# Queries on all partitions: selecting matmuls out of PSUM, or repeated loads from a DRAM scratch

## The chip, the cores and the metric

The kernel runs on one core of a Trainium2 chip. The core has TensorE (matmuls, written PE; its weight loads PEld), VectorE (DVE), ScalarE (ACT), GpSimd (POOL) and SyncE (SP), whose queue issues most of the loads and stores, and 16 DMA engines that carry them out. Each engine works through its own list of instructions in order; semaphores hold an instruction back until what it needs is there. The metric is the device time of one execution in microseconds (us), the median of several.

## The reference

One layer of a decoder step is computed for a prompt of 512 tokens and for a sample group: 8 sequences of 8 new tokens, each with its own cache. The part that matters here is the dilated attention of the sample group, for three groups of four heads with (window, dilation) = (128, 1), (512, 4) and (2048, 16):

```python
def dilated_attention_sample(q, k_ext, v_ext, window, dil, slopes):
    # q: (B,L,Hg,E); k_ext, v_ext: window buffer rows, then the L new rows
    span = window // dil
    jj = np.arange(span + 1)
    idx = wb + np.arange(l_len)[:, None] - jj[None, :] * dil
    ...
    s = jnp.einsum('blhe,bljhe->blhj', q, kg) * (e ** -0.5)
    s = jnp.where(valid[None, :, None, :], s + bias, NEG_INF)
    p, den, lse = _softmax_parts(s, -1)
    o = jnp.einsum('blhj,bljhe->blhe', p, vg) / den
    return o, lse[..., 0]
```

With dilation 16 and 8 new tokens, the token i of a sequence reads the cached rows whose position has residue i modulo 16: 128 keys of four heads of 64 elements. No two of the eight tokens share a cached key. The outputs of the three groups are weighted by a softmax over their denominators and go through further projections.

## The kernel before

The core holds activations with features on the partitions and 576 tokens (512 of the prompt, 64 of the sample group) on the free axis. Nearly all matmuls are projections in `products` (L231): weights and activations are split into a high and a low part of fp32r, and each product is made of three matmuls. Weights come in chunks of 512 KB by SyncE (L164) into three buffers; ScalarE casts the high part (L148) and VectorE subtracts to get the low part (L150). L423 is the same scheme for values that come out with tokens on the partitions.

The attention stage goes over the groups in the order 2, 1, 0. For each it projects the queries, keys and values of all tokens, and then makes the prompt's units (`part_scores`, L833 to L840; `part_values`, L848 to L859) in turn with steps of the sample group, which a generator hands out (`all_samples`). What an engine does in which order is settled when the program is built: a scheduler there puts the instructions of the code into one list for each engine and may draw projections that are written later, such as the gate projections `gc` (written behind the whole stage), between the steps of the attention, where they fill TensorE while it would wait.

Group 2's sample scores (`scores_by_query`) are not made by TensorE, since every token has its own keys. For each quad of sequences `bq` (two) and each token's residue r (eight), `unit` loads a tile `kv` of 128 keys on the partitions by 4 sequences by 256 elements (512 KB, L870). Each half of it (two sequences) is multiplied element by element with the token's query, which must stand on all 128 partitions, and summed over each head's 64 elements into `sT` (L917). TensorE puts the query there: `qhl` holds the queries' rows, token by partition, in a high part on partitions 0 to 63 and a low part on 64 to 127, and `sel` has two ones in each column. A matmul with one column of `sel`, repeated 128 times, as weights (L909) writes the sum of the two rows on all partitions of a PSUM bank. For the first half VectorE multiplies straight out of PSUM (L916); for the second ScalarE copies PSUM into `qr` (L913) and GpSimd multiplies (L914). VectorE makes the sums of both. The tiles `qr` share a tag, and so three buffers, with `skT` of the other groups. Behind the eighth residue, `sT` is transposed (L940), the bias is added and the minimum taken (`minus_max`, L819), ScalarE takes exponentials (L945), and two transposes (L947, L948) turn them for the product with the values (L955, L964). The products are masked into `od` (L968) and summed into `orow` (L969).

At the end of the stage the last quad of group 0 goes through these steps, while the prompt's group weights `ae` are turned by transposes (L1083) and multiplied into the prompt's outputs (L1085); the sample group's weights are applied to `orow` (L1088), three transposes (L1091) turn it, and its parts go into `oun`. From `oun` come the high and low parts `och` and `ocl` (L1113) for the projection behind the stage.

`small()` hands out PSUM banks: in turns, each fifth one by the name h (shared with `held()`) and the others by the name s; in the attention stage only those named s. Line numbers in the text are those of the kernel before, save where the kernel after is spoken of; there they are 5 less in the sample steps (L947 is L942), 10 less from L1027 on, and 1 more in the prompt's units.

Of the kernel before, what the change touches and what calls it, by code (L numbers as in the profile page):

```python
# [104 lines left out]
def hybrid_step(ctx: ExitStack, tc: tile.TileContext, I, O, at_a, at_b):  # L105
# [707 lines left out]
    nat = oup.tile([128, 4, 3, 2, 4], F32, name="nat")  # L813
    stp = oup.tile([128, 4, 2, 2, 4], F32, name="stp")
    scr = dpool.tile([512, 16], F32, name="scr")

    def minus_max(out, scores, bias, least):

# [82 lines left out]
    def scores_by_query(sT, bq):  # L901

        for r in range(NR[2]):
            kt = unit(2, bq, r, 0)
            for half in range(2):
                pq = small()
                for n in range(2):
                    tok = 8 * (4 * bq + 2 * half + n) + r
                    T.matmul(pq[:, 256 * n:256 * n + 256], sel[:, tok:tok + 1].to_broadcast([128, 128]), qhl, start=True, stop=True)  # L909
                k2 = kt[:, 2 * half:2 * half + 2, :].rearrange("p b f -> p (b f)")  # L910
                if half:
                    qr = sa.tile([128, 512], F32, tag="skT", name="qr", bufs=3)
                    S.copy(qr, pq)  # L913
                    G.tensor_tensor(k2, k2, qr, op=OP.mult)  # L914
                else:
                    V.tensor_tensor(k2, k2, pq, op=OP.mult)  # L916
                V.tensor_reduce(sT.rearrange("p (b h i) -> p b h i", b=4, h=4)[:, 2 * half:2 * half + 2, :, r],  # L917
                                k2.rearrange("p (b h e) -> p b h e", b=2, h=4), axis=AX.X, op=OP.add)
            yield
# [71 lines left out]
    for g in GROUPS:  # L991
# [19 lines left out]
        if g == 2:  # L1011
            pt = small()
            for p in range(2):
                qd = sa.tile([128, 2, 64], F32, tag="qd", name="qd", bufs=1)
                for d in range(2):
                    V.tensor_copy(qd[:, d, :], qs[:, 4 + p, :])
                T.transpose(pt[:, 128 * p:128 * p + 128], qd.rearrange("p d n -> p (d n)"), ident)
            qhl = sa.tile([128, 256], F32R, tag="qhl", name="qhl")
            S.copy(qhl, pt[:, :256])
            V.tensor_tensor(qhl[64:128], pt[64:128, :256], qhl[64:128].bitcast(F32), op=OP.subtract)  # L1020
            sel = sa.tile([128, 64], F32R, tag="sel", name="sel")
            V.tensor_tensor(sel, ident[:, 0:64], ident[:, 64:128], op=OP.add)

        for _ in prompt_units(g, qT, kT, vt):
            for _ in range(STEPS[g]):
# [490 lines left out]
```

## Time and profile before

| | us |
|---|---|
| median of 3 runs | 1310.12 (1309.93 to 1310.55) |
| the profiled execution's own time | 1309.6 |
| its span, first to last instruction | 1307.6 |
| TensorE's granted clock, mean | 0.997 |

A row of the profile names the line of the kernel, the engine, the operation and the tiles (out<-in), the count and the durations. Rows of one line give the shortest, median and longest duration in ns, then the first and last start in us. Matmuls overlap in TensorE, so the duration of one is longer than the distance to the next. A chain of waits is read back from the last instruction: each piece is what the end waited for at that time. The busiest lines of the page's second part, the span in 40 slices, show how evenly TensorE is filled (tenths of each slice):

```profile
PE   8899999999999999999999999999999999999996
DMA  7241432376573767355767432563556656545423
```

The attention stage with its sample steps lies in slices 15 to 24.

### The profile page before, as it was taken

Reading aid. Unit: us, or ns where it says so; the run is one execution under the profiler, and the core shown is the slowest. Engines: PE = TensorE matmul, PEld = TensorE weight load, DVE = VectorE, ACT = ScalarE, POOL = GpSimd, SP = SyncE. Lnnn points to the kernel's source line nnn. Section 1 sums busy time; section 2 is a strip of 40 time slices with the busy share of each in tenths; the row PEclk is TensorE's granted clock in tenths of the full one; section 3 lists DMA queues with packets and bytes.
Section 4 is the critical chain, followed back from the end, with each engine's and each line's share of the span. In section 5 each row is a group of like instructions: output and inputs, shape, how many; then the busy total and the mean of one; then the engine's idle time right before and its main releaser. Section 6 shows DMA issues by size and latency. Waiting matters only on the chain.

```text
span 1307.6 us, 24226 instructions
## 1 busy us (share of the span) xinstructions
PE 1279.0 (98%) x9699; PEld 1227.7 (94%) x9699; DVE 685.3 (52%) x1294; ACT 573.1 (44%) x1262; POOL 251.1 (19%) x400
## 2 busy tenths in 40 slices
PE   8899999999999999999999999999999999999996
PEld 6899999999999999998988879999989999999996
DVE  5855564343463223171624357545898888773233
ACT  6554553544432222252533334444456666553333
POOL 4320211013420222041312101022232222200000
PEclk9999999999999999999999999999999999999999
DMA  7241432376573767355767432563556656545423
GB/s 221 65 133 53 146 118 69 97 232 192 163 250 91 244 218 257 95 172 166 227 191 216 139 93 81 157 223 107 160 149 155 138 136 150 116 112 142 137 77 117
DMA packets 225484, 196.39 MB, mean 150 GB/s; under 512 B 8444, under 2 KB 216937, under 8 KB 224596
## 3 DMA queue, kind: packets, MB, share of 16 engines
q1 hardware_dynamic: 218682, 142.28, 37.4%
q0 software_dynamic: 6688, 52.57, 13.4%
q8 instruction: 76, 1.25, 0.4%
q14 instruction: 36, 0.29, 0.1%
q10 hardware_dynamic: 2, 0.00, 0.0%
HBM read 175.52 MB, written 54.27 MB: 176 GB/s over the span
## 4 chain that ended last, share of the span: by engine, by line
PE 83%; issue 5%; DVE 5%; ACT 4%; DMA 2%; SPq 0%; POOL 0%; POOLq 0%; ACTq 0%; DVEq 0%
PE g L231 44%; PE g L1430 8%; PE g L423 7%; PE g L1273 6%; PE s L1273 3%; PE s L1430 2%; DMA wr<-wr 1%; PE h L964 1%; PE s L833 1%; DVE wl L150 1%; PE h L1273 1%; PE s L231 1%; PE s L909 1%; PE s L892 1%; PE s L848 1%
## 5 line engine op out<-in xcount | busy, mean ns | idle before, releaser
L150 DVE TENSOR_TENSOR wl<-wr,wh 128x512 fp32r<-128x512 f32 (+2 forms) x286 | 201.8, 708 | 324.4 <-ACT wh L148 305.4
L231 PE MATMUL g<-xh,wh 128*128 128x288 f32 (+2 forms) x1120 | 334.7, 299 | 3.1 <-DVE ae L1319 1.6
L231 PE MATMUL g<-xh,wl 128*128 128x288 f32 (+2 forms) x1120 | 334.0, 298 | 0.5 <-DVE wl L150 0.5
L231 PE MATMUL g<-xl,wh 128*128 128x288 f32 (+2 forms) x1120 | 332.7, 297 | 0.1
L148 ACT CAST wh<-wr 128x512 fp32r<-128x512 f32 (+2 forms) x290 | 174.8, 607 | 341.4 <-PE g L231 229.8
L231 PEld LDWEIGHTS g<-xh,wh 128*128 128x128 f32 x1120 | 211.8, 189 | 7.3 <-issue 3.8
L231 PEld LDWEIGHTS g<-xh,wl 128*128 128x128 f32 x1120 | 211.6, 189 | 1.8 <-DVE wl L150 0.8
L231 PEld LDWEIGHTS g<-xl,wh 128*128 128x128 f32 x1120 | 211.6, 189 | 1.7 <-issue 1.1
L1233 DVE TENSOR_TENSOR wl<-wr,wh 128x512 fp32r<-128x512 f32 x119 | 81.3, 707 | 22.2 <-ACT wh L1232 22.0
L1232 ACT CAST wh<-wr 128x512 fp32r<-128x512 f32 x119 | 70.3, 620 | 45.5 <-DVE wr L1224 23.1
L423 PE MATMUL g<-wh,xh 128*128 128x256 f32 x224 | 71.1, 318 | 2.8 <-DVE vs L428 2.8
L1430 PE MATMUL g<-hh,wh 128*128 128x288 f32 (+2 forms) x286 | 71.3, 297 | 0.2 <-ACT hh L1244 0.2
L1430 PE MATMUL g<-hh,wl 128*128 128x288 f32 (+2 forms) x286 | 71.2, 297 | 0.0
L423 PE MATMUL g<-wl,xh 128*128 128x256 f32 x224 | 71.1, 318 | 0.0
L423 PE MATMUL g<-wh,xl 128*128 128x256 f32 x224 | 70.9, 317 | 0.0
L1430 PE MATMUL g<-hl,wh 128*128 128x288 f32 (+2 forms) x286 | 70.7, 296 | 0.0
L1273 PE MATMUL g<-xh_t,wh 128*128 128x288 f32 x204 | 60.5, 297 | 0.6 <-DVE h L1366 0.4
L1273 PE MATMUL g<-xh_t,wl 128*128 128x288 f32 x204 | 60.3, 295 | 0.0
L1273 PE MATMUL g<-xl_t,wh 128*128 128x288 f32 x204 | 59.9, 294 | 0.0
L423 PEld LDWEIGHTS g<-wh,xh 128*128 128x128 f32 x224 | 51.6, 230 | 4.1 <-DVE vs L428 3.0
L423 PEld LDWEIGHTS g<-wl,xh 128*128 128x128 f32 x224 | 51.6, 230 | 1.2 <-issue 1.2
L423 PEld LDWEIGHTS g<-wh,xl 128*128 128x128 f32 x224 | 51.6, 230 | 1.2 <-issue 1.2
(520 smaller groups left out, 2987.6 us busy)
## 6 DMA issues: line engine op xcount, KB each, us to landing
wr<-in_w_in_dram SPq DMA_DIRECT2D x74, 512.0 KB
wr<-in_ffn_w_up_dram SPq DMA_DIRECT2D x44, 512.0 KB
out_dram<-in_cache_k_w_dram POOLq DMA_DIRECT2D x8, 2040.0 KB, 9.6
out_dram<-in_cache_v_w_dram POOLq DMA_DIRECT2D x8, 2040.0 KB, 9.8
kv<-in_cache_k_w_dram SPq DMA_DIRECT2D x26, 512.0 KB
kv<-in_cache_v_w_dram SPq DMA_DIRECT2D x26, 512.0 KB
wr<-wr POOLq DMA_DIRECT2D x34, 256.0 KB, 3.7
wr<-in_ffn_w_down_dram SPq DMA_DIRECT2D x18, 448.0 KB
```

What stands on the lines that cost most here:

```text
L148: S.copy(hi[:, :n], src)
L150: return hi, lo, E.tensor_tensor(lo[:, :n], src, hi[:, :n].bitcast(F32), op=OP.subtract)
L231: T.matmul(ps[:, :t1 - t0], a, b(n)[:, t0:t1], start=(n == 0 and j == 0), stop=(n == len(ks) - 1 and j == 2))
L423: mm = T.matmul(dst, a, b, start=(n == 0 and j == 0), stop=(n == 7 and j == len(seq) - 1))
L833: T.matmul(sp[:, nk * n:nk * n + nk], qT[r, p, 128 * t:128 * t + 128], kT[r, p, k0:k0 + nk], start=True, stop=True)
L848: T.transpose(pt[:, 128 * n:128 * n + 128], s4[:, h, 128 * kb:128 * kb + 128], ident)
L892: T.transpose(pk[:, 128 * n:128 * n + 128], kt[:, 2 * half + n // 2, 128 * (n % 2):128 * (n % 2) + 128], ident)
L909: T.matmul(pq[:, 256 * n:256 * n + 256], sel[:, tok:tok + 1].to_broadcast([128, 128]), qhl, start=True, stop=True)
L1232: S.copy(hi, src)
L1233: V.tensor_tensor(lo, src, f32(hi), op=OP.subtract)
L1273: T.matmul(ps, a[:, 128 * k:128 * k + 128], b[:, k, :], start=start and k == 0 and j == 0, stop=k == 3 and j == 2, skip_group_check=True)
L1430: T.matmul(q[:, :t1 - t0], a, b[n][:, t0:t1], start=(n == 0 and j == 0), stop=(n == NF - 1 and j == 2))
```

## The change

The queries of group 2 are transposed without doubling (64 rows out), copied by ScalarE into `qt` and stored by SyncE into a DRAM scratch `qrow` of 64 rows by 256 elements. For each half of each residue, SyncE loads two rows (two sequences, one token) from the scratch, repeated over all 128 partitions: 256 KB written into the tile `qr`. VectorE multiplies the first half and GpSimd the second, both with `qr` from SBUF. The 64 selecting matmuls, ScalarE's 16 copies of PSUM, and the tiles `qhl`, `sel` and `qd` are gone. All 32 tiles `qr` now go through the three buffers of their tag. SyncE's list grows by 33 transfers.

```diff
+    qrow = dpool.tile([64, 256], F32, name="qrow")
...
         for r in range(NR[2]):
             kt = unit(2, bq, r, 0)
             for half in range(2):
-                pq = small()
-                for n in range(2):
-                    tok = 8 * (4 * bq + 2 * half + n) + r
-                    T.matmul(pq[:, 256 * n:256 * n + 256], sel[:, tok:tok + 1].to_broadcast([128, 128]), qhl, start=True, stop=True)
+                qr = sa.tile([128, 2, 256], F32, tag="skT", name="qr", bufs=3)
+                b0 = 4 * bq + 2 * half
+                nc.sync.dma_start(qr, qrow.rearrange("(b i) f -> i b f", i=8)[r, b0:b0 + 2][None].to_broadcast([128, 2, 256]))
                 k2 = kt[:, 2 * half:2 * half + 2, :].rearrange("p b f -> p (b f)")
-                if half:
-                    qr = sa.tile([128, 512], F32, tag="skT", name="qr", bufs=3)
-                    S.copy(qr, pq)
-                    G.tensor_tensor(k2, k2, qr, op=OP.mult)
-                else:
-                    V.tensor_tensor(k2, k2, pq, op=OP.mult)
+                (G if half else V).tensor_tensor(k2, k2, qr.rearrange("p b f -> p (b f)"), op=OP.mult)
...
         if g == 2:
             pt = small()
             for p in range(2):
-                qd = sa.tile([128, 2, 64], F32, tag="qd", name="qd", bufs=1)
-                for d in range(2):
-                    V.tensor_copy(qd[:, d, :], qs[:, 4 + p, :])
-                T.transpose(pt[:, 128 * p:128 * p + 128], qd.rearrange("p d n -> p (d n)"), ident)
-            qhl = sa.tile([128, 256], F32R, tag="qhl", name="qhl")
-            S.copy(qhl, pt[:, :256])
-            V.tensor_tensor(qhl[64:128], pt[64:128, :256], qhl[64:128].bitcast(F32), op=OP.subtract)
-            sel = sa.tile([128, 64], F32R, tag="sel", name="sel")
-            V.tensor_tensor(sel, ident[:, 0:64], ident[:, 64:128], op=OP.add)
+                T.transpose(pt[:64, 128 * p:128 * p + 128], qs[:, 4 + p, :], ident)
+            qt = sa.tile([64, 256], F32, name="qt")
+            S.copy(qt, pt[:64, :256])
+            nc.sync.dma_start(qrow, qt)
```

The order of two engines is needed below. SyncE's list before, from the store of group 2's prompt values (`av`) on, which lies at the beginning of the first quad (`wr` are weight chunks, `kv` tiles of the cache):

```order
L1049 DMA out_dram<-av 128x1024
L164 DMA wr<-in_w_in_dram 128x4x256 x2
L870 DMA kv<-in_cache_k_w_dram 128x4x256 x4
L164 DMA wr<-in_w_in_dram 128x8x128
L870 DMA kv<-in_cache_v_w_dram 128x4x256 x2
```

and the same place in the kernel after:

```order
L1039 DMA out_dram<-av 128x1024
L1012 DMA qrow<-qt 64x256
L164 DMA wr<-in_w_in_dram 128x4x256
L909 DMA qr<-qrow 128x2x256 x6
L871 DMA kv<-in_cache_k_w_dram 128x4x256
L909 DMA qr<-qrow 128x2x256
L164 DMA wr<-in_w_in_dram 128x4x256
L909 DMA qr<-qrow 128x2x256 x2
L871 DMA kv<-in_cache_k_w_dram 128x4x256 x2
```

The store of the scratch and six loads from it now stand ahead of the next cache tile, and the second weight chunk stands behind seven of them, where it followed the first at once.

TensorE's list before, at the end of the attention stage. Ahead of these rows are the last raw scores of group 0 (L897), four matmuls of L856 and 20 more of L231; `ss` are the exponentials, `ae` the prompt's group weights, `ak` and `ksn` the new keys on their way out:

```order
L231 MATMUL g<-xl,wh 128x288
L231 MATMUL g<-xh,wl 128x288
L947 MATMUL s<-ca,ss 128x128
L948 MATMUL s<-ca,ss 64x128
L1037 MATMUL s<-ca,ak 128x128 x2
L1042 MATMUL s<-ca,ksn 64x128 x2
L1083 MATMUL s<-ca,ae 128x128 x4
L231 MATMUL g<-xh,wh 128x288
L231 MATMUL g<-xl,wh 128x288
L231 MATMUL g<-xh,wl 128x288
L955 MATMUL h<-vsn_5713,ptn 128x256
L964 MATMUL h<-kv,ptc 32x256 x4
```

and after, with the last raw scores (L898) among the rows:

```order
L857 MATMUL s<-pts,av 64x128 x4
L933 MATMUL h<-ksn,qb 128x64 x2
L898 MATMUL h<-skT,qb 32x128 x8
L942 MATMUL s<-ca,ss 128x128
L943 MATMUL s<-ca,ss 64x128
L1027 MATMUL s<-ca,ak 128x128 x2
L1032 MATMUL s<-ca,ksn 64x128 x2
L1073 MATMUL s<-ca,ae 128x128 x4
L950 MATMUL h<-vsn_5713,ptn 128x256
L959 MATMUL h<-kv,ptc 32x256 x4
L1073 MATMUL s<-ca,ae 128x128 x8
L1073 MATMUL h<-ca,ae 128x128 x4
```

The L231 matmuls, which belong to the gate projections, stand earlier in the list now, and the transposes of the exponentials (L942, L943) follow the raw scores (L898) directly. In both lists 24 matmuls of L231 stand between the turning of `orow` and the first matmul that reads `och`.

## The prediction

> **What bounds the kernel now.** I read the page first: the busy line and the chain of work that ended last, by engine.
>
> ```profile
> span 1307.6 us, 24226 instructions
> PE 1279.0 (98%) x9699; PEld 1227.7 (94%) x9699; DVE 685.3 (52%) x1294; ACT 573.1 (44%) x1262; POOL 251.1 (19%) x400
> PE 83%; issue 5%; DVE 5%; ACT 4%; DMA 2%; SPq 0%; POOL 0%; POOLq 0%; ACTq 0%; DVEq 0%
> ```
>
> TensorE is busy for 98% of the span and carries 83% of the chain, so instructions taken off TensorE are worth their pitch, provided that nothing else is late where they stood. Whether that holds is a question of the stage. The windows (length, busy time of each engine with its count, the granted TensorE clock, DMA share and GB/s) cover the two stretches in which group 2's scores are computed, one for each quad of sequences, and the end of the attention stage.
>
> ```profile
> 560.00:580.00 20.00, 20.00 (x159) 19.35 (x158) 14.89 (x31) 10.02 (x26) 8.04 (x9) 1.00 0.58 179
> 620.00:640.00 20.00, 20.00 (x145) 18.40 (x145) 12.20 (x34) 9.39 (x30) 4.86 (x8) 1.00 0.80 241
> 760.00:780.00 20.00, 20.00 (x176) 17.41 (x174) 9.55 (x30) 8.42 (x20) 0.00 (x0) 1.00 0.16 48
> 780.00:800.00 20.00, 18.58 (x133) 17.01 (x132) 16.43 (x30) 9.26 (x21) 5.49 (x5) 1.00 0.15 43
> ```
>
> TensorE has no gap up to 780 us and its clock is full. The first gaps, 20 − 18.58 = 1.4 us, come at the end of the stage, where the last softmax and the weighting of the groups run. VectorE is the next engine (14.89 of 20), and the DMA engines are over half busy.
>
> **What goes from TensorE.** The selecting matmuls are one group of the trace; the chain of waits gives their pitch.
>
> ```profile
> L909 PE MATMUL s<-qhl,sel x64: 274/279/384, 563.2 to 654.2; 128*128 128x256 f32 x64
> 563.31 0.92 PE s L909 x8
> 564.24 2.52 PE g L231 x20
> 566.76 0.47 PE s L909 x4
> 639.84 0.89 PE s L909 x6
> ```
>
> A matmul lasts 0.28 us, but they overlap: 0.92/8 = 0.47/4 = 0.117 us each in the first quad, and up to 0.148 (0.89/6) in the second. 64 × 0.117 = 7.5 us. I take the low pitch, since a longer one in the chain includes time that a neighbour will take over. The two transposes that prepared the queries stay. Term 1: **−7.5 us**.
>
> **What goes from and comes to the other engines.**
>
> ```profile
> L916 DVE TENSOR_TENSOR kv<-kv,s x16: 666/682/689, 563.6 to 654.3; 128x512 f32<-128x512 f32 x16
> L917 DVE TENSOR_REDUCE sT<-kv x32: 666/677/691, 564.8 to 656.8; 128x8 f32<-128x512 f32 x32
> L913 ACT COPY qr<-s x16: 586/587/592, 563.8 to 654.6; 128x512 f32<-128x512 f32 x16
> L914 POOL TENSOR_TENSOR kv<-kv,qr x16: 1277/1293/1492, 564.5 to 655.2; 128x512 f32<-128x512 f32 x16
> ```
>
> The 32 multiplies and 32 reductions stay on their engines; VectorE's 16 multiplies now read both inputs from SBUF. ScalarE loses 16 × 0.587 = 9.4 us, beside TensorE's work, so nothing by itself. VectorE's small preparing operations go too, at the start and hidden.
>
> New are 33 DMAs of SyncE's queue: one store of 64 KB and 32 loads of 256 KB (8.4 MB). The trace has both kinds of step elsewhere: a round trip through a DRAM scratch (L1053, L1054), and one row put on all partitions (L1457, 4 KB a partition, 512 KB), with the windows around it.
>
> ```profile
> L1053 SPq DMA_DIRECT2D scr<-stp x1: 339/339/339, 667.4 to 667.4; - x1
> L1054 SPq DMA_DIRECT2D nat<-scr x1: 377/377/377, 670.2 to 670.2; - x1
> L1457 SPq DMA_DIRECT2D yx<-in_final_norm_g_dram x1: 363/363/363, 1169.2 to 1169.2; - x1
> 1170.00:1171.00 1.00, 1.00 (x10) 1.00 (x9) 1.00 (x2) 0.91 (x2) 0.00 (x0) 1.00 0.77 193
> 1171.00:1172.00 1.00, 1.00 (x9) 1.00 (x9) 1.00 (x3) 0.00 (x0) 0.00 (x0) 1.00 0.84 299
> 1172.00:1173.00 1.00, 1.00 (x10) 1.00 (x9) 1.00 (x3) 0.00 (x0) 0.00 (x0) 1.00 0.08 33
> ```
>
> Store to load: 670.2 − 667.4 = 2.8 us. The repeated row occupied the DMA engines for 0.77 + 0.84 + 0.08 = 1.7 us and was done by 1172.1, some 2.9 us after its issue began; half its bytes save 0.85 us of engine time, so about 2.1 to 2.9 us for one quiet load of 256 KB, and I take 2.6. Pieces of 1 KB are half of that row's longest contiguous stretch, so this may be too good; the bounds are below.
>
> Now the ring. The store is issued at 557.3 (where the old order had its first group-2 rows, TensorE at 555.9), lands at 560.1, the first load at 562.7. Three buffers, and each goes round in issue and landing (0.4 + 2.6) plus a multiply (0.68 or 1.29) and its signals (some 0.5): about 4.6 us a round, 1.5 us a load. Sixteen loads of a quad end at about 562.7 + 15 × 1.55 = 586. The transpose of `sT`, which needs all of them, stands in the new order behind rows that, added up by their pitches, reach 599.3. That is a slack of 12 us. But VectorE works in order, and behind its reductions stand, in the new order, the copy of the prompt's probabilities that L857's matmuls need (572.6 by the same sum; the rows show copy and matmuls before, there L856), and the splits of weights for L231.
>
> ```profile
> 573.70 0.68 DVE L851 COPY pts<-s 128x512 f32<-128x512 f32 x1
> 576.54 0.59 PE s L856 x8
> ```
>
> The copy follows two rounds: landed by 568.1, multiplied and reduced by about 570.6, copied by 571.3, it has 1.3 us left. By the same count the weight split behind the fifth round has 2.6 us; in the second quad the smallest slack is 3. If the landing takes x longer than 2.6, the stall of the first quad is about the larger of 2x − 1.3 and 5x − 2.6.
>
> Bounds on x. Below: 0, the quiet row. Above: the DMA engines are not quiet here.
>
> ```profile
> 570.00:580.00 10.00, 10.00 (x82) 9.35 (x81) 7.48 (x20) 5.36 (x16) 2.66 (x3) 1.00 0.91 289
> wr<-wr POOLq DMA_DIRECT2D x34, 256.0 KB, 3.7
> ```
>
> From 560 to 590 they moved some 5.5 MB; 16 loads add 4.2 MB, 9.7 MB in 30 us or 320 GB/s, more than the 289 GB/s that this stretch shows at a share of 0.91. The 256 KB transfers of GpSimd's queue have a median of 3.7 us from issue to landing among such traffic: x = 1.1, stall 5.5 − 2.6 = 2.9 us. The ring itself spreads the loads over 25 us, and the K tiles and weights behind it in SyncE's queue mostly wait for buffers anyway, so I take x nearer to the quiet row: x = 0.7, 5 × 0.7 − 2.6 = 0.9. Term 2: **+1 us** (0 to 2.9).
>
> A weight load that stood ahead of group 2's loads now stands between them on SyncE. It goes out at about 568, as it did before, and the split that needs it stands at 588 on TensorE's time, so I count nothing; cover lost, it would cost its delay beyond some 17 us.
>
> **What is late next: the tail.** The order of the end of the stage changes too. Before, between the last raw scores (L897) and the transposes of their exponentials (L947), TensorE had 4 + 22 other matmuls; in the new order these gate matmuls run earlier and L942 follows L898 directly; three more went from ahead of L955. What they covered:
>
> ```profile
> 773.38 0.36 DVE L819 CUSTOM_DVE_ANT_0 ss<-h,cbs 128x192 f32<-128x192 f32 x1 [1.24 <-PE h L897]
> 773.78 0.46 ACT L945 ACTIVATE ss<-ss,smx 128x192 f32<-128x192 f32 x1 [0.97 <-DVE smx L819]
> 774.15 0.19 ACT L945 ACTIVATION_READ_ACCUMULATOR ss<-ss,smx 128x1 f32 x1
> PE s L1091 <- DVE orow L1088: 0.8, 1, 0.8
> PE h L1083 <- ACT ae L1079: 0.3, 1, 0.3
> PE g L231 <- POOL ocl L1113: 0.2, 1, 0.2
> L968 DVE TENSOR_TENSOR od<-h,ca x6: 404/425/426, 627.5 to 779.7; 128x256 f32<-128x256 f32 x6
> L969 DVE TENSOR_REDUCE orow<-od x6: 584/604/628, 628.4 to 780.9; 128x64 f32<-128x256 f32 x6
> L1088 DVE TENSOR_TENSOR orow<-orow,sgw x1: 550/550/550, 782.6 to 782.6; 128x384 f32<-128x384 f32 x1
> ```
>
> From the minimum's start to the exponentials' end it is 774.34 − 773.38 = 1.0 us, with signals about 1.3, now bare. Behind that, `od`, its sum and the weighting (0.43 + 0.60 + 0.55 = 1.6 us, with VectorE's other multiplies between) are covered by the same group of transposes as before, and I estimate 1.2 us of waiting there, and 0.2 at the end as before. 2.7 against the 0.8 + 0.3 + 0.2 = 1.3 of before. Term 3: **+1.4 us** (0, if VectorE and ScalarE run ahead of TensorE, to 3).
>
> **Sum.** 1309.6 for the profiled execution (span 1307.6 and 2.0 around it), − 7.5 + 1.0 + 1.4 = 1304.5. The median is 0.5 above the profiled execution, so **1305.0 us**.
>
> **Rivals.**
>
> *A lock between VectorE and GpSimd.* Before, VectorE's multiply had one input in PSUM.
>
> ```profile
> 565.99 1.58 DVE L150 TENSOR_TENSOR wl<-wr,wh 128x512 fp32r<-128x512 f32 x1
> 569.29 0.67 DVE L916 TENSOR_TENSOR kv<-kv,s 128x512 f32<-128x512 f32 x1
> 564.49 2.54 POOL L914 TENSOR_TENSOR kv<-kv,qr 128x512 f32<-128x512 f32 x2 [6.55 <-ACT qr L913]
> 568.84 2.54 POOL L914 TENSOR_TENSOR kv<-kv,qr 128x512 f32<-128x512 f32 x2
> ```
>
> Beside GpSimd's multiplies the weight split, both of whose inputs are in SBUF, took 1.58 us where it usually takes about 0.69; the multiply out of PSUM kept its 0.67. So a multiply from SBUF beside one of GpSimd's may cost 0.9 us more: at worst 8 × 0.9 = 7 us a quad, less the slacks of 2.6 and 3, about 4.5 and 4, or 8.5 us of stall: 1304 + 8.5, about 1312 us. Against it: 8 GpSimd multiplies of 1.29 us fill only 10 of some 25 us of a quad. [...]
>
> *The ring falls behind (slower).* With x = 1.75 the first quad's stall is 5 × 1.75 − 2.6 = 6.1 us and all of the gain that terms 1 and 3 leave is gone: the point is an issue-to-landing time of about 4.4 us. At 6 us (x = 3.4) it is 14.4, and 5 more in the second quad: 1305 − 1 + 19, about 1323 us; a spread of 1315 to 1325. For it speaks the GB/s above, against it that 3.7 is the median of loads of this size, queued on a busy queue.
>
> *Landings of about 4 us:* stalls of 3 to 7 us, 1307.5 to 1312.
>
> *Nothing is late at all:* terms 2 and 3 vanish, 1310.1 − 7.5 = 1302.5.
>
> That the change doesn't do what it says is excluded by the order: no row of L909's matmuls is left on TensorE.
>
> **How the numbers follow.** The forecast (1303.5 to 1306) gets 0.52, nothing late 0.10, landings of 4 us 0.17, the lock 0.08, the ring behind 0.13. A measurement of this kernel tells about 0.2%, 2.6 us, from no change. Faster than that (under 1307.5): 0.52 + 0.10 + 0.04 of the landings = 0.66. Within: 0.13 of the landings and 0.05 of the lock = 0.18. Slower (over 1312.7): the ring and 0.03 of the lock = 0.16. The range of 8 in 10 runs from 1302, below the full gain, to 1311.5, so that it leaves out the ring and most of the lock.
>
> **What will show it.** In the changed profile: no idle TensorE at 556 to 670 (term 2 right) or waits of L857, L231 or L935 that end with VectorE or a DMA (wrong); issue to landing of the `qr` loads near 3.3 us (wrong from 4.4); TensorE's waits at the end of the stage of about 2.7 us in all; VectorE's multiplies at 0.68 us, or at 1.3 and more where the lock holds. A TensorE busy time that falls by other than some 7 us, or a gap in the later stages, where I count no change, would make the prediction wrong in a way that I don't foresee.

## The result, and the profile after

| | us |
|---|---|
| before, median of 4 | 1310.34 (1309.93 to 1311.39) |
| after, median of 4 | 1343.27 (1340.47 to 1344.84) |
| ratio | 1.0244, 95% interval 1.023 to 1.0258 |
| the profiled execution after | 1344.7, span 1342.8 |

The change makes the kernel 33 us slower; the prediction had 1305.0, and 1311.5 at the upper end of its range.

The page of the kernel after, and its windows over the same stretches and the ones behind them (columns as before: length, busy time of PE, PEld, DVE, ACT, POOL, granted clock, DMA share, GB/s):

```profile
span 1342.8 us, 24113 instructions
PE 1286.0 (96%) x9635; PEld 1231.8 (92%) x9635; DVE 686.5 (51%) x1288; ACT 563.3 (42%) x1246; POOL 252.6 (19%) x400
```

```profile
560.00:580.00 20.00, 14.53 (x116) 13.58 (x116) 10.13 (x24) 6.50 (x26) 3.40 (x4) 0.95 0.71 125
580.00:600.00 20.00, 17.42 (x114) 16.44 (x111) 8.28 (x13) 6.12 (x15) 5.86 (x6) 0.88 0.81 220
600.00:620.00 20.00, 12.76 (x55) 12.47 (x56) 6.71 (x11) 0.00 (x0) 4.32 (x7) 0.74 0.92 235
...
640.00:660.00 20.00, 19.95 (x157) 17.54 (x156) 9.49 (x29) 8.12 (x28) 4.87 (x8) 1.00 0.80 213
660.00:680.00 20.00, 15.94 (x103) 15.64 (x104) 9.75 (x21) 6.80 (x21) 3.88 (x3) 0.83 0.87 233
680.00:700.00 20.00, 12.71 (x83) 12.11 (x81) 8.09 (x14) 1.90 (x5) 3.80 (x3) 0.83 0.89 222
700.00:720.00 20.00, 19.46 (x164) 15.37 (x165) 6.00 (x19) 8.05 (x24) 3.57 (x8) 0.91 0.74 213
```

TensorE, which had no gap here before, now sits idle for 5.47 + 2.58 + 7.24 us in the first quad and for 0.05 + 4.06 + 7.29 + 0.54 in the second, 27.2 us in all. And its granted clock, 1.00 throughout before, falls to 0.74 to 0.95 in all of these windows but the one from 640 to 660. Where the DMA engines were 0.91 busy before they moved 289 GB/s; now 0.92 goes with 235, and 0.71 with 125.

What TensorE waited for between 540 and 860 us (engine, line, releaser; us in total, times, longest), then what VectorE's multiplies and the loads of `qr` show:

```profile
PE g L423 <- DVE wl L150: 13.9, 5, 5.6
PE s L857 <- ACT as L838: 5.5, 1, 5.5
PE s L857 <- DVE pts L852: 4.1, 1, 4.1
PE h L935 <- DVE sT L912: 2.3, 1, 2.3
...
PE s L942 <- ACT ss L940: 1.1, 1, 1.1
PE s L1073 <- ACT ae L1069: 0.8, 1, 0.8
PE h L1081 <- DVE orow L1078: 0.3, 1, 0.3
...
PE g L231 <- POOL ocl L1103: 0.2, 1, 0.2
```

```profile
DVE kv L911 <- DMA qr<-qrow: 30.9, 13, 4.8
DVE sT L912 <- POOL kv L911: 20.8, 8, 3.6
```

```profile
L909 SPq DMA_DIRECT2D qr<-qrow x32: 359/437/2991, 561.0 to 688.7; - x32
...
L911 DVE TENSOR_TENSOR kv<-kv,qr x16: 691/692/1180, 567.7 to 695.4; 128x512 f32<-128x512 f32 x16
```

The names that TensorE waits for are VectorE and ScalarE, but VectorE itself waits 30.9 us for loads of `qr`, and another 20.8 for GpSimd's multiplies, which wait for such loads too. The weight splits (L150) and the copies of probabilities (L852) that TensorE needs stand behind them in VectorE's list. The longest wait for a split in the second quad shows it: ScalarE's cast of that half chunk (L148) is done at 680.3 us, the split comes 8 us later, directly behind a multiply that waited for its load, and TensorE, idle from 684.6 on, goes on when the split ends.

```profile
679.67 0.62 ACT L148 CAST wh<-wr 128x512 fp32r<-128x512 f32 x1 [1.23 <-PE g L231]
688.00 0.69 DVE L911 TENSOR_TENSOR kv<-kv,qr 128x512 f32<-128x512 f32 x1 [4.82 <-DMA qr<-qrow]
688.61 0.68 DVE L150 TENSOR_TENSOR wl<-wr,wh 128x512 fp32r<-128x512 f32 x1
```

The first load is issued at 561.0 and the first multiply starts at 567.7: 6.7 us, where the prediction had some 3.3. (For the first 1.4 us of it the weight chunk ahead was still coming in.) The multiplies themselves take 0.69 us, as before.

The DMA view of a stretch in which little else moves shows the rate of these loads:

```profile
DMA packets 345, 0.34 MB, mean 84 GB/s; under 512 B 17, under 2 KB 345, under 8 KB 345
q1 hardware_dynamic: 345, 0.34, 90.4%
```

Between 564 and 568 us, 345 pieces of (nearly all) 1 KB occupied 16 engines for 90.4% of 4 us: 57.9 / 345 = 168 ns a piece. The same view of the kernel before, while the cache's tiles came in (570 to 575, also pieces of 1 KB):

```profile
DMA packets 1764, 1.76 MB, mean 351 GB/s; under 512 B 50, under 2 KB 1764, under 8 KB 1764
q1 hardware_dynamic: 1764, 1.76, 107.0%
```

That is 48.5 ns a piece. A load of `qr` has 256 pieces, so it needs 256 x 168 / 16 = 2.7 us of all 16 engines, and a quad's sixteen need 43 us, with the cache and the weights beside them. The question for the experiments is why the same bytes in the same pieces are 3.5 times slower.

### The profile page after: what moved, and what is told of

Read it like the earlier page. It is cut to its first block, busy times and chain, and to the rows that moved or that the text cites. A ratio compares the mean times of both kernels' runs of the same rounds, so it can differ in the third digit from the quotient of the medians.

```text
span 1342.8 us, 24113 instructions
## 1 busy us (share of the span) xinstructions
PE 1286.0 (96%) x9635; PEld 1231.8 (92%) x9635; DVE 686.5 (51%) x1288; ACT 563.3 (42%) x1246; POOL 252.6 (19%) x400
## 5 line engine op out<-in xcount | busy, mean ns | idle before, releaser
L150 DVE TENSOR_TENSOR wl<-wr,wh 128x512 fp32r<-128x512 f32 (+2 forms) x286 | 202.3, 711 | 303.7 <-ACT wh L148 295.4
L231 PE MATMUL g<-xh,wh 128*128 128x288 f32 (+2 forms) x1120 | 335.8, 300 | 3.1 <-DVE ae L1309 1.6
L231 PE MATMUL g<-xh,wl 128*128 128x288 f32 (+2 forms) x1120 | 336.0, 300 | 1.2 <-DVE wl L150 1.2
L231 PE MATMUL g<-xl,wh 128*128 128x288 f32 (+2 forms) x1120 | 335.7, 300 | 0.1
L148 ACT CAST wh<-wr 128x512 fp32r<-128x512 f32 (+2 forms) x290 | 174.9, 606 | 337.0 <-PE g L231 230.3
L231 PEld LDWEIGHTS g<-xh,wh 128*128 128x128 f32 x1120 | 213.3, 190 | 5.8 <-issue 2.2
L231 PEld LDWEIGHTS g<-xh,wl 128*128 128x128 f32 x1120 | 213.4, 190 | 4.4 <-issue 2.6
L231 PEld LDWEIGHTS g<-xl,wh 128*128 128x128 f32 x1120 | 213.4, 191 | 3.3 <-issue 2.4
```

Source lines behind the costliest of these rows:

```text
L148: S.copy(hi[:, :n], src)
L150: return hi, lo, E.tensor_tensor(lo[:, :n], src, hi[:, :n].bitcast(F32), op=OP.subtract)
L231: T.matmul(ps[:, :t1 - t0], a, b(n)[:, t0:t1], start=(n == 0 and j == 0), stop=(n == len(ks) - 1 and j == 2))
```

## The experiments

The times of the kernel before in the same jobs were 1310.7, 1311.0 and 1311.2 us (medians of 19 to 21).

**Side by side: pieces of 2 KB.**

```diff
-                nc.sync.dma_start(qr, qrow.rearrange("(b i) f -> i b f", i=8)[r, b0:b0 + 2][None].to_broadcast([128, 2, 256]))
+                nc.sync.dma_start(qr.rearrange("p b f -> p (b f)"), qrow.rearrange("(i b) f -> i (b f)", b=8)[r, 256 * b0:256 * b0 + 512][None].to_broadcast([128, 512]))
...
-                T.transpose(pt[:64, 128 * p:128 * p + 128], qs[:, 4 + p, :], ident)
+                qp = sa.tile([128, 64], F32, tag="od", name="qp", bufs=1)
+                V.tensor_copy(qp.rearrange("p (i b) -> p i b", i=8), qs[:, 4 + p, :].rearrange("p (b i) -> p i b", b=8))
+                T.transpose(pt[:64, 128 * p:128 * p + 128], qp, ident)
```

> The scratch is written with its rows in the order token, sequence, so that the two rows of a load lie side by side: a load of qr is 128 pieces of 2 KB instead of 256 of 1 KB, all else as in the change. In the changed kernel 345 pieces of 1 KB took 168 ns each (90.4% of 16 engines for 4 us), and the quiet row of 4 KB pieces in the kernel before some 210 ns each. Theory A, that a repeated source costs a nearly fixed time for each piece (some 170 to 210 ns up to 4 KB): the DMA engines need 1.4 to 1.7 us for a load instead of 2.7, so about half of the 35 us are gone, 1312 to 1325 us. Rival B, that a repeated source is limited in bytes (some 85 GB/s): 330 ns a piece, 1335 to 1345 us. Rival C, that the whole added traffic of 8.4 MB is too much whatever its source: 1335 to 1345 us.

Measured: 1312.74 us (1308.73 to 1315.98), ratio 1.001 (0.9996 to 1.0023). Putting the two rows of a load side by side in the scratch, which also makes one piece of 2 KB out of two of 1 KB, takes back 30 of the 33 us. The first load is multiplied 3.3 us after its issue (564.2 to 567.5), as the prediction had it. The traffic as such (rival C) is not the cause, nor is a limit of 85 GB/s for anything that is repeated (rival B). The time is where theory A put it, but the stretch from 566 to 568 us is not:

```profile
DMA packets 331, 0.60 MB, mean 301 GB/s; under 512 B 37, under 2 KB 37, under 8 KB 331
q1 hardware_dynamic: 331, 0.60, 81.0%
```

25.9 us of engine time for 331 pieces are 78 ns each: a piece of 2 KB took less than half as long as one of 1 KB. A fixed time for each piece can't do that.

**Sixteen copies of the scratch, 64 KB apart.**

```diff
-    qrow = dpool.tile([64, 256], F32, name="qrow")
+    qrow = dpool.tile([1024, 256], F32, name="qrow")
...
+                rows = qrow.rearrange("(c i b) f -> i c (b f)", c=16, b=8)[r, :, 256 * b0:256 * b0 + 512]
+                nc.sync.dma_start(qr.rearrange("p b f -> p (b f)"), rows[:, None].to_broadcast([16, 8, 512]))
...
-            nc.sync.dma_start(qrow, qt)
+            nc.sync.dma_start(qrow.rearrange("(c n) f -> n c f", c=16), qt[:, None, :].to_broadcast([64, 16, 256]))
```

> As e1_2kb, and the scratch holds 16 copies (one store of 1 MB), of which each group of 8 partitions reads its own. Theory A in the form that pieces from one place wait for each other: a piece of 2 KB comes down to about twice the 48.5 ns that a 1 KB piece of the cache took before, 100 ns, a load needs 0.8 us of the 16 engines, and the time is 1303 to 1312 us. If each piece is slow because it is read again at all, or because it comes from a scratch: as e1_2kb. Rival C (too much traffic): above 1330 us.

Measured: 1328.77 us, ratio 1.0133 (1.0116 to 1.015), 16 us worse than one copy. Part of it is the store: from 564 to 568 the DMA engines were 98.3% busy with it at 189 GB/s, and the first load went out at 568.9 instead of 564.2. But the loads are slower too, 227 GB/s between 570.5 and 573.5. The form of theory A in which readers of one place wait for each other finds no support here. It isn't refuted either: should places 64 KB apart share a limit, as places 8 KB apart turn out to below, the copies don't test it.

**Every piece from a place of its own.**

```diff
-                nc.sync.dma_start(qr, qrow.rearrange("(b i) f -> i b f", i=8)[r, b0:b0 + 2][None].to_broadcast([128, 2, 256]))
+                nc.sync.dma_start(qr, I[KEYS[2][1]][0, b0:b0 + 2].rearrange("b (m r) h e -> r m b (h e)", r=16)[r])
```

> Each load of qr reads 256 pieces of 1 KB from 256 different places (the value cache, in the pattern of the cache tiles) instead of two rows of the scratch; the scores are made with these rows instead of the queries. The bytes, the pieces, the queue, the buffers and the waits stay as in the change. Theory A (a place read again is slow): about 50 ns a piece, 0.8 us of 16 engines for a load, 1303 to 1315 us. Rival C (traffic, three buffers, SyncE's queue): within 5 us of the change, 1338 to 1349 us.

Measured: 1301.37 us (two runs), ratio 0.9929 (0.9909 to 0.9949). With 256 different places the same number of bytes and pieces through the same three buffers costs TensorE next to nothing (one wait of 0.7 us for a weight split), and the kernel gains 9.4 us. It proves less than it seems, though: these loads don't depend on the store, and the scheduler began them at 513.4 us, 48 us earlier than in the change.

**One load for all multiplies.**

```diff
+    one = []
...
-                qr = sa.tile([128, 2, 256], F32, tag="skT", name="qr", bufs=3)
-                b0 = 4 * bq + 2 * half
-                nc.sync.dma_start(qr, qrow.rearrange("(b i) f -> i b f", i=8)[r, b0:b0 + 2][None].to_broadcast([128, 2, 256]))
+                qr = one[0]
...
             nc.sync.dma_start(qrow, qt)
+            one.append(sa.tile([128, 2, 256], F32, tag="skT", name="qr", bufs=3))
+            nc.sync.dma_start(one[0], qrow.rearrange("(b i) f -> i b f", i=8)[0, 0:2][None].to_broadcast([128, 2, 256]))
```

> One tile qr is loaded once and all 32 multiplies read it, so all tokens get the same query; the loads in the ring are gone, everything else of the change stays (no selecting matmuls, multiplies out of SBUF on VectorE and GpSimd, the other order at the end of the stage). By terms 1 and 3 of the prediction: 1310.3 - 7.5 + 1.4 = about 1304 us, within 2 us. If the loss comes from VectorE's and GpSimd's multiplies blocking each other, or from the new order, and not from the loads: above 1312 us.

Measured: 1309.02 us (1305.87 to 1312.01, ten runs), ratio 0.9986 (0.9976 to 0.9997): between the two expectations. So the loads carry the loss of the change, but without them the gain of 6 us doesn't appear either. The timeline of VectorE and GpSimd in its profiled execution (at 1312.0 us the longest of the ten) shows why (start, us, instruction, count, idle before), and its windows what followed:

```profile
566.51 6.92 DVE L911 TENSOR_TENSOR kv<-kv,qr 128x512 f32<-128x512 f32 x4 [1.66 <-DMA qr<-qrow]
```

```profile
566.50 6.37 POOL L911 TENSOR_TENSOR kv<-kv,qr 128x512 f32<-128x512 f32 x4 [6.12 <-DMA qr<-qrow]
```

```profile
577.00:579.00 2.00, 0.31 (x3) 0.10 (x1) 2.00 (x6) 0.00 (x0) 0.60 (x1) 1.00 0.65 189
579.00:581.00 2.00, 0.63 (x6) 0.66 (x8) 2.00 (x9) 1.92 (x8) 0.72 (x2) 0.64 0.91 251
581.00:583.00 2.00, 2.00 (x13) 1.67 (x10) 2.00 (x3) 1.67 (x6) 1.56 (x1) 0.50 1.01 309
583.00:585.00 2.00, 2.00 (x11) 2.00 (x10) 2.00 (x5) 0.38 (x1) 0.00 (x0) 0.50 1.03 356
585.00:587.00 2.00, 2.00 (x11) 2.00 (x11) 2.00 (x2) 0.00 (x0) 1.95 (x2) 0.65 0.50 135
```

With nothing to pace them, four multiplies of VectorE and four of GpSimd run against each other: 6.92 / 4 = 1.73 us each on VectorE instead of 0.69, and 6.37 / 4 = 1.59 on GpSimd instead of 1.28. That is what the prediction held as a rival under the name of a lock; the rows show that the multiplies are longer side by side, not what makes them so. It puts VectorE 4.2 us back, and TensorE idles for 1.69 + 1.37 = 3.1 us. In the change itself the loads keep the multiplies apart (median 0.692, longest 1.18), so there the lock is no cause worth counting. The second lesson of these rows is the clock: after the idle 3 us it is at half for 6.8 us, and up to 2 x 0.36 + 4 x 0.5 + 2 x 0.35 = 3.4 us of work are lost on top of the gap.

**Two rows 2 KB apart.** The first four runs left two theories: the distance of the two rows (8 KB in the change, 64 KB between copies), or the small repeated piece.

```diff
-                T.transpose(pt[:64, 128 * p:128 * p + 128], qs[:, 4 + p, :], ident)
+                qp = sa.tile([128, 64], F32, tag="od", name="qp", bufs=1)
+                for q in range(2):
+                    for n in range(2):
+                        V.tensor_copy(qp.rearrange("p (i q n h) -> p i q n h", i=8, q=2, n=2)[:, :, q, n, :],
+                                      qs[:, 4 + p, :].rearrange("p (q h n i) -> p i q h n", q=2, h=2, n=2)[:, :, q, :, n])
+                T.transpose(pt[:64, 128 * p:128 * p + 128], qp, ident)
...
-                nc.sync.dma_start(qr, qrow.rearrange("(b i) f -> i b f", i=8)[r, b0:b0 + 2][None].to_broadcast([128, 2, 256]))
+                nc.sync.dma_start(qr, qrow.rearrange("(i q n h) f -> i q h n f", i=8, q=2, n=2)[r, bq, half][None].to_broadcast([128, 2, 256]))
```

> The scratch's rows are put in the order token, quad, sequence, half, so that the two rows of a load lie 2 KB apart (8 KB in the change, side by side in e1_2kb); a load is 256 pieces of 1 KB again. The pure stretches so far: 168 ns for a repeated piece of 1 KB in the change, 78 ns (81.0% of 16 engines for 2 us, 331 pieces) for one of 2 KB in e1_2kb. Theory D, that the distance of the two places that alternate is what is slow (8 KB, and 64 KB in e2_16copies): at 2 KB a 1 KB piece falls to about 50 ns and the time is near e1_2kb's, 1308 to 1318 us. Rival P, that repeated pieces of 1 KB are slow by their size or their alternation, whatever the distance: 168 ns a piece and 1338 to 1348 us.

Measured: 1316.14 us (1311.96 to 1318.67), ratio 1.0035 (1.0022 to 1.0047). From 566 to 568 us:

```profile
DMA packets 578, 0.56 MB, mean 279 GB/s; under 512 B 34, under 2 KB 578, under 8 KB 578
q1 hardware_dynamic: 578, 0.56, 94.8%
```

52 ns for a repeated piece of 1 KB, as theory D said. Small repeated pieces are not slow by their size, and rival P falls.

**One row.**

```diff
-                nc.sync.dma_start(qr, qrow.rearrange("(b i) f -> i b f", i=8)[r, b0:b0 + 2][None].to_broadcast([128, 2, 256]))
+                nc.sync.dma_start(qr, qrow.rearrange("(b i) f -> i b f", i=8)[r, b0:b0 + 1][None].to_broadcast([128, 2, 256]))
```

> Each load repeats one row of 1 KB 256 times instead of two rows 128 times each; the second sequence of a pair gets the query of the first. Pieces of 1 KB, one place. Theory D, and any theory by which the alternation of two places is slow: about 50 ns a piece and 1308 to 1318 us. Rival P, by which it is the small repeated piece: about 168 ns a piece and 1338 to 1348 us.

Measured: 1347.97 us, one run. It went against theory D: with no alternation at all the loads are as slow as in the change. The stretch from 570 to 578 us:

```profile
DMA packets 692, 0.67 MB, mean 84 GB/s; under 512 B 38, under 2 KB 692, under 8 KB 692
q1 hardware_dynamic: 692, 0.67, 49.9%
```

84 GB/s again, with the DMA engines only half busy. So the limit is not in the engines: it lies with what is read. The theory that is left: **what one kilobyte of the scratch can deliver is some 85 GB/s, and a repeated load is as fast as the neighbouring kilobytes that it, with the loads beside it, spreads over.** Two rows 8 KB apart count as one. Just ahead of this stretch, from 567 to 570 us, the loads ran at 153 to 192 GB/s, in the change from 568 to 570 at 164. By the order of the loads the third, which begins the next token, joins the second there, and its rows lie one kilobyte on from the first one's; that fits the theory, but the trace doesn't tell which row a piece read. The theory was made to fit the rates so far; the rates of the further runs, below, fit it as well.

**Sixteen copies, 65 KB apart.**

```diff
-    qrow = dpool.tile([64, 256], F32, name="qrow")
+    qrow = dpool.tile([1040, 256], F32, name="qrow")
...
+                rows = qrow.rearrange("(c n) f -> c n f", c=16)[:, 8 * r + b0:8 * r + b0 + 2].rearrange("c b f -> c (b f)")
+                nc.sync.dma_start(qr.rearrange("p b f -> p (b f)"), rows[:, None].to_broadcast([16, 8, 512]))
...
-            nc.sync.dma_start(qrow, qt)
+            nc.sync.dma_start(qrow.rearrange("(c n) f -> n c f", c=16)[0:64], qt[:, None, :].to_broadcast([64, 16, 256]))
```

> As e2_16copies (16 copies, pieces of 2 KB, one copy for each group of 8 partitions), but the copies lie 65 KB apart instead of 64. In e2_16copies a piece took about 110 ns (81.8% of 16 engines for 3 us, 370 pieces) and the time was 1328.8 us. Theory D in the form that places at a power of two of distance share something that serves one at a time: about 80 ns or less a piece, and the store of 1 MB faster than the 189 GB/s there, 1308 to 1316 us. Rival, that the copies cost what they cost because of the store of 1 MB and the later start of the ring: within 5 us of e2_16copies.

Measured: 1324.03 us (two runs), ratio 1.0097 (1.0077 to 1.0117): within 5 us of the copies 64 KB apart, as the rival said. The loads had 282 GB/s between 569 and 571, against 191 between 570.5 and 572 with 64 KB, which fits the theory; but the store of 1 MB ran at the same 181 to 194 GB/s, held the ring back to 567.6, and ate what the copies could give. Copies don't pay here, and how much of their time is the distance's and how much the store's wasn't separated.

**Half and half.** The lines that differ from the kernel after in the multiplies; the block that prepares the queries, which makes both `qhl` and the scratch, is left out.

```diff
...
+                if half:
+                    b0 = 4 * bq + 2
+                    qr = sa.tile([128, 512], F32, tag="skT", name="qr", bufs=3)
+                    nc.sync.dma_start(qr, qrow.rearrange("(i b) f -> i (b f)", b=8)[r, 256 * b0:256 * b0 + 512][None].to_broadcast([128, 512]))
+                    G.tensor_tensor(k2, k2, qr, op=OP.mult)
+                else:
+                    pq = small()
+                    for n in range(2):
+                        tok = 8 * r + 4 * bq + n
+                        T.matmul(pq[:, 256 * n:256 * n + 256], sel[:, tok:tok + 1].to_broadcast([128, 128]), qhl, start=True, stop=True)
+                    V.tensor_tensor(k2, k2, pq, op=OP.mult)
...
```

> The kernel before, with the loads (in pieces of 2 KB) for the second half of each tile alone, where they take the place of ScalarE's copy; the first half keeps its selecting matmuls and VectorE's multiply out of PSUM. 32 matmuls go (3.7 us of TensorE), 16 loads or 4.2 MB come, VectorE and GpSimd no longer both read two SBUF inputs, and there are 18 matmuls left between the last raw scores and the transposes of the exponentials. If the loads in pieces of 2 KB are quick enough when there are half as many: 1310.5 - 3.7 = 1306 to 1308 us. If VectorE's line still waits for GpSimd's late multiplies: 1309 to 1313 us.

Measured: 1308.59 us (1306.42 to 1311.23, ten runs), ratio 0.9983 (0.9974 to 0.9993): a gain of 2.4 us by the medians, a little less than expected. It holds the cleanest rate of one place of 2 KB, since successive loads here go to places 8 KB apart (566 to 569 us):

```profile
DMA packets 285, 0.53 MB, mean 178 GB/s; under 512 B 32, under 2 KB 32, under 8 KB 284
```

**An earlier ring.** In the run with pieces of 2 KB side by side, TensorE still idled 2 to 3 us in each quad (1.95 in the first, 1.96 + 0.44 + 0.38 in the second), with the DMA engines at 1.03 of their time between 580 and 600 us and at 0.14 between 540 and 560. The block that turns and stores the queries was moved from behind the projection of the values to right behind the last projection of the queries.

```diff
                 gemm(P[nm, 2 * g + p], XH, XL, evac, SPLIT)
+                if g == 2 and (nm, p) == ("qa", 1):
+                    pt = small()
+                    for pp in range(2):
+                        qp = sa.tile([128, 64], F32, tag="od", name="qp", bufs=1)
+                        V.tensor_copy(qp.rearrange("p (i b) -> p i b", i=8), qs[:, 4 + pp, :].rearrange("p (b i) -> p i b", b=8))
+                        T.transpose(pt[:64, 128 * pp:128 * pp + 128], qp, ident)
+                    qt = sa.tile([64, 256], F32, name="qt")
+                    S.copy(qt, pt[:64, :256])
+                    nc.sync.dma_start(qrow, qt)
...
```

> e1_2kb with the turning and storing of the queries moved ahead, right behind the projection that makes the last of them, some 15 us earlier. The ring can start while the DMA engines are at 0.14 (540 to 560) instead of filling them to 1.0 (574 to 603 in e1_2kb). Theory: in e1_2kb what is left of the loss is the traffic of the ring in too short a time, with the idle TensorE (2 us a quad) and the lower granted clock behind each; so with the early start the first quad's gap goes: 1306 to 1309 us where e1_2kb had 1312.7 and the kernel before 1310.7. Rival: it is the late port or VectorE's line of multiplies and sums, which an early start only shifts: 1311 to 1315 us.

Measured: **1298.78 us** (1297.52 to 1300.99, four runs), ratio 0.9907 (0.9892 to 0.9922). It is faster than both kernels, and by more than expected. Its windows and its waits of TensorE from 480 to 820 us:

```profile
540.00:560.00 20.00, 20.00 (x101) 19.75 (x100) 10.18 (x20) 4.96 (x12) 5.14 (x5) 1.00 0.74 233
560.00:580.00 20.00, 20.00 (x163) 19.20 (x162) 12.83 (x37) 9.80 (x34) 5.98 (x8) 1.00 0.94 290
580.00:600.00 20.00, 20.00 (x182) 15.76 (x180) 5.82 (x18) 8.41 (x26) 4.91 (x12) 1.00 0.65 196
...
620.00:640.00 20.00, 20.00 (x160) 18.41 (x160) 15.19 (x45) 11.13 (x37) 6.02 (x8) 1.00 0.92 293
```

```profile
PE s L1075 <- ACT ae L1071: 0.8, 1, 0.8
PE h L1083 <- DVE orow L1080: 0.3, 1, 0.3
PE g L231 <- POOL ocl L1105: 0.2, 1, 0.2
```

No gap in either quad, and a full clock: the loads, the first of which now goes out at 533.9 us, 30 us earlier than in the run with the late store and not the 15 that were expected, begin in the stretch that was nearly empty. The first matmul behind the attention stage that reads `och` starts at 777.78 instead of 786.84 us, 9.1 us earlier, which is most of the 10.7 us by which the span is shorter (1296.9 against 1307.6). Counted matmul by matmul, this run was 1.8 us behind the kernel before at 511 us, ahead of anything that the edit touches, so that the stage itself gained 10.8 us.

**The early ring with the slow places, and half and half with them.** Two runs cross the two causes: the change with the store moved ahead as above and its rows 8 KB apart as they were, and half and half with rows 8 KB apart (the line of the change in place of the one with 2 KB). The early store was also tried on half and half with pieces of 2 KB.

> The change itself with the earlier store, places 8 KB apart as in the change (84 to 89 GB/s). Theory, that the rate of the repeated loads sets the ring (2.7 us or more a load, 43 us and more a quad): the first quad gains at most the 15 us of the earlier start, the second nothing: 1325 to 1338 us. If the loss of the change came from the late start of the ring alone: as e9_early2kb.

Measured: 1325.27 us (two runs), ratio 1.0106 (1.0088 to 1.0125). Of the gaps ahead, 5.6 us are left (L849 and L857), and TensorE now waits 13.4 us for `sT` itself (L935), in two waits. The four corners are: late and 8 KB apart 1343.3, early and 8 KB apart 1325.3, late and side by side 1312.7, early and side by side 1298.8. The place is worth 27 to 31 us, the start 14 to 18.

> e8_hybrid with the scratch of the change, rows 8 KB apart, 16 loads at 84 to 89 GB/s instead of 176: half the dose of the slow loads, 8 x 3 = 24 us a quad, about the time that a quad has. Theory of the rate: a small loss against e8_hybrid, 1309 to 1318 us. If each slow load cost TensorE its own share (35 us for 32): half of the loss, about 1324 us or more.

Measured: 1314.66 us, ratio 1.0027 (1.0017 to 1.0037), 6 us more than with pieces of 2 KB, and no half of the loss: sixteen slow loads nearly fit in the time that two quads have, thirty-two don't. The loss sets in at a rate, not at each load.

> e8_hybrid with the same earlier turning and storing. e8_hybrid had only 0.5 us of idle TensorE in the ring, so there is little to win: 1306 to 1308.6 us; if the earlier loads push weights back in SyncE's queue: above 1309 us.

Measured: 1308.4 us (eleven runs), ratio 0.998 (0.9971 to 0.9988), as expected the same as half and half without it.

## Why the prediction was wrong, step by step

- **Term 1, the removed matmuls, was right in kind and too small.** Where nothing is in the way the end of the attention stage comes 9.1 us earlier, not 7.5. The pitch of 0.117 us was that of the first quad; the chain of waits showed up to 0.148 in the second, and I put the excess down to neighbours. The 10.8 us that the stage gained are more than even 64 x 0.148 = 9.5, so some of the gain isn't the pitch of these matmuls; what it is, no run shows.
- **Term 2 failed, and with it the sign.** The step was "half its bytes save 0.85 us of engine time, so about 2.1 to 2.9 us for one quiet load ... and I take 2.6". It carried the speed of a row of 4 KB over to rows of 1 KB. The measured rates of repeated loads are 84 GB/s for one place of 1 KB, 84 for two of them 8 KB apart, 178 for one place of 2 KB, and 279 to 301 where successive loads together cover 4 KB; the row of the prediction, 4 KB, had 299 in its fastest microsecond. Even the caveat was off: 1 KB is a quarter of that row's stretch of 4 KB, not half. From issue to the first multiply it took 6.7 us, and a quad's sixteen loads needed 43 us of the engines, where the prediction's ring had 25 us for them. With rows side by side the first load took the 3.3 us that were foreseen: the price was right for a place of the row's width, and wrong for the scratch as it was laid out. (No run shows the prediction's 0.5 us for signals in each round. The one of them that the trace of the kernel after shows is short: the multiply that starts at 567.74 and takes 0.69 us ends at 568.43, and the next load of `qr` is issued at 568.46.)
- **The way from x to the stall held, its size partly by luck.** The copies and splits that TensorE needs did stand behind the late multiplies in VectorE's list. With x = 6.7 - 2.6 = 4.1 the prediction's formula gives 5 x 4.1 - 2.6 = 18 us for the first quad, and scaling its second-quad figure (5 us at 3.4) by 5 for each us of x gives 8.5; together 26.5. The windows show 27.2 of idle TensorE, split 15.3 and 11.9: the quads are off by 2.7 and 3.4 us in opposite directions, so that the sum fits better than its parts, and x is that of the first load alone, which had a weight chunk ahead of it. The rival "the ring falls behind" is what happened; no run tests its decision point of 4.4 us. It got 0.13, since the 3.7 us of another queue's transfers stood nearest, and its time, 1315 to 1325, was too low.
- **A term was missing: the granted clock.** From 1309.6 the removed 9.1 us, the 27.2 us of gaps and 1.2 us at the end of the stage lead to 1328.9; the profiled execution took 1344.7. Most of the other 15.8 us is the clock. In the windows from 560 to 720 us it averages 0.89, which over 160 us is 17 us of lost clock, and by the trace 13.6 us of it fall on time in which TensorE was at work. The last 2 us stay open; the 9.1 us, read off another run, are no more exact than that. The prediction priced a stall at its length; here it cost half as much again.
- **Term 3 was right.** At the end of the stage TensorE waits 1.1 + 0.8 + 0.3 + 0.2 = 2.4 us by the waits and 2.6 by the windows (2.22 + 0.35 from 800 to 840), against 2.7 predicted and 1.4 before, with the wait for the exponentials (L942, 1.1 us) where the prediction put it.
- **The lock between VectorE and GpSimd** showed itself where both run freely (one load for all multiplies), at 1.73 us a multiply instead of 0.69, and was no cause in the change, where the median is 0.692. That it would cost little there was right, for a reason that the prediction didn't give: slow loads kept the two apart.
- **The weight load behind the ring** was costed at nothing, and that held, though TensorE's longest total wait is for weight splits (L150, 13.9 us). In the two longest of these waits the weights had long come: ScalarE's casts were done at 596.5 and 680.3 us, and the splits came at 609.7 and 688.6, behind multiplies that waited for `qr`. They are part of term 2. With rows side by side and nearly the same order of SyncE's list these waits are 3.9 us, and with the early ring none.
- A slip without weight: "nothing is late" is 1310.1 − 7.5 = 1302.6, not 1302.5.

## What to carry to other kernels

A load that repeats a short row over all partitions was not priced by its bytes or its pieces here: it came at 84 GB/s from one kilobyte, at 178 from two side by side, and at 279 to 301 where successive loads covered four. Look at how many neighbouring kilobytes of DRAM the loads in flight cover, and lay the scratch out so that successive loads read side by side. A load that nothing but a store holds back belongs as early as its data exist, where the time ahead of a busy stage is free, as here (the DMA engines were at 0.14 from 540 to 560 us). And a gap in a bound TensorE can cost more than its length: behind some of the gaps of 1.95 to 5.5 us in these runs the granted clock was at half for 3.4 or 6.8 us.

## What the hardware showed that was not expected

- The limit of a repeated read lies at its source: at 84 GB/s the 16 DMA engines were once 90% and once 50% busy. Rows 8 KB apart were no faster than one row; rows 2 KB apart, where two successive loads cover 4 KB, were three times as fast, while the cache's tiles, pieces of 1 KB that are 16 KB apart, came at 351 GB/s without repeats. What in the memory makes a kilobyte and its neighbour 8 KB on share a limit, and over which distances, is open; the runs tell the rule for this scratch alone.
- The clock behind a gap. In the kernel after, TensorE idles for 5.5 us until 579.7; then:

```profile
578.00:580.00 2.00, 0.29 (x4) 0.32 (x6) 2.00 (x7) 1.92 (x10) 0.00 (x0) 0.50 0.90 196
580.00:582.00 2.00, 2.00 (x13) 1.67 (x10) 0.56 (x2) 1.06 (x2) 1.71 (x3) 0.50 1.13 325
582.00:584.00 2.00, 2.00 (x11) 2.00 (x11) 0.29 (x1) 1.01 (x3) 0.39 (x1) 0.50 1.02 189
584.00:586.00 2.00, 2.00 (x16) 2.00 (x16) 1.18 (x2) 0.00 (x0) 0.00 (x0) 0.81 0.65 206
```

  Half speed lasts from 577.9 to 584.8 us, 6.8 us, of which some 5 are full work. Every stretch at half speed between 500 and 860 us in this trace lasts 3.4 or 6.8 us; there are six. Shorter gaps did it too: 3.1 us in the run with one load (a clock of 0.64, 0.50, 0.50 and 0.65 in the windows from 579 to 587 us, which is 6.8 us at half), and 1.95 and 1.96 us in the run with pieces of 2 KB (the first from 592.4 us, with 0.84, 0.50 and 0.81 in the windows from 594 to 600, 3.4 us at half; the second between 660 and 680 us, where the mean is 0.91). Other gaps of that size did not: in the run with two rows 2 KB apart TensorE idles for 3.3 us between 640 and 660 us, in one wait for ScalarE (L857 <- L838), and the clock is 1.00 there and up to 720 us; and in the early ring with the slow places waits of 2.3 and 3.3 us between 560 and 580 us go with a mean of 0.91, which is about one stretch of 3.4 us for both. So the length of a gap alone doesn't settle what the clock does behind it; what else does, no run shows.
